# Softmax on one core: two of eight input chunks loaded from ScalarE's store queue, and a larger share of the scaling on ScalarE

## The chip, the cores and the metric

The kernel runs on 1 core of one Trainium2 chip. The metric is the device time of one execution in microseconds (us). Three runs of the kernel before gave 161.81, 161.76 and 161.81 us, so the median is 161.81 us.

## The reference

The input x is float32 of shape 16 x 1024 x 512. The output is a softmax over the last axis with temperature 0.5:

```python
x_scaled = x / 0.5
x_max = np.max(x_scaled, axis=-1, keepdims=True)
exp_x = np.exp(x_scaled - x_max)
return exp_x / np.sum(exp_x, axis=-1, keepdims=True)
```

That is 16384 independent rows of 512 numbers: 33.55 MB are read and 33.55 MB are written.

## The kernel before, in words

**Chunks.** The 16384 rows are cut into eight chunks (`C` = 8) of 128 partitions x `G` = 16 rows, so a chunk is a tile of 128 x 16 x 512 floats, 4096 KB, and each partition's part of it is 32 KB that lie together in memory. Six tiles (`BUFS` = 6) hold chunks; chunks 6 and 7 reuse the tiles of chunks 0 and 1 and can be loaded only after those have been stored. Everything is done in place in these tiles.

**Blocks.** The compute works on blocks of a chunk (`BLOCKS`): chunk 0 is cut in blocks of 4, 4 and 8 rows, chunk 7 in two of 8, and the other chunks are one block of 16 rows. There are eleven blocks. For a block, three engines' queues do this:

- VectorE (DVE) takes the maximum of each row (L77, one instruction for the block) and makes the bias from it (L81). This is the function `shift`.
- ScalarE (ACT) does one instruction per row (L108, `exponentials`), which writes the exponentials in place and their sum into `sums`.
- VectorE inverts the sums (L125) and multiplies the first `k = b - b // 8` of the block's b rows by them (L127, `scale_vector`). ScalarE multiplies the remaining `b // 8` rows, one instruction each (L138, `scale_scalar`). So of 16 rows VectorE scales 14 and ScalarE 2; of 8 rows 7 and 1; of 4 rows 4 and 0.
- When the last block of a chunk is scaled, ScalarE's queue issues the chunk's store (L148, `store`), one DMA of 4096 KB per chunk.

**Loads.** All loads but one small one are issued from SyncE's queue (SP, L68), in the order of the chunks: chunk 0 in two parts of 4 and 12 rows (1024 KB and 3072 KB; "0a" and "0b" below), then chunks 1 to 5 whole, with no wait between them; then chunk 6, which waits until the store of chunk 0 has landed, and chunk 7 without its last row, which waits for the store of chunk 1. The last row of chunk 7 comes from GpSimd's queue (POOL, L97) in two small DMAs.

**Order of work.** The order on each engine is written out by hand (`tc.manual_schedule()`), by the loop at the end of the kernel:

```python
for i in range(n):
    if i + 1 < n:
        exponentials(i + 1, rows(i + 1)[0])
    scale_vector(i)
    scale_scalar(i)
    if i + 2 < n:
        shift(i + 2)
    store(i)
    if i + 1 < n:
        exponentials(i + 1, rows(i + 1)[1])
```

So VectorE does: maximum of block i+1, inverse and scaling of block i, maximum of block i+2, and so on. ScalarE does: the exponentials of block i+1, its share of the scaling of block i, the issue of the store, and the next exponentials. A store that is not ready holds ScalarE. `rows` splits the exponentials of chunk 1 alone: 14 rows come ahead of the store of chunk 0 and 2 rows behind it. A load is issued (on SP, which has nothing else to do) when `shift` first asks for its chunk.

Of the kernel before, what the change touches and what calls it, by code (L numbers as in the profile page):

```python
# [1 line left out]

# [4 lines left out]


@with_exitstack
def kernel(  # L10
    ctx: ExitStack,
    tc: tile.TileContext,
    x: bass.AP,
    out: bass.AP,
):
    nc = tc.nc
    fp32 = mybir.dt.float32
    P = nc.NUM_PARTITIONS
    AX = mybir.AxisListType.X
    EXP = mybir.ActivationFunctionType.Exp  # L20
    COPY = mybir.ActivationFunctionType.Copy
    MAX = mybir.AluOpType.max

    D = x.shape[-1]
    xf = x.flatten_outer_dims()
    of = out.flatten_outer_dims()
    N = xf.shape[0]

    G = 16
    C = N // (P * G)
    assert C * P * G == N
    xr = xf.rearrange("(c p g) d -> c p g d", p=P, g=G)
    outr = of.rearrange("(c p g) d -> c p g d", p=P, g=G)
    WHOLE = [(0, G)]
    LOADS = [[(0, 4), (4, G)]] + [WHOLE] * 6 + [[(0, G - 1)]]
    BLOCKS = [[(0, 4), (4, 8), (8, G)]] + [WHOLE] * 6 + [[(0, 8), (8, G)]]
    STORES = [WHOLE] * 8  # L40
    BMAX = 16
    BUFS = 6

    data = ctx.enter_context(tc.tile_pool(name="data", bufs=BUFS))
    stats = ctx.enter_context(tc.tile_pool(name="stats", bufs=6))

    ctx.enter_context(tc.manual_schedule())


    warm = stats.tile([P, 1], fp32, name="warm", bufs=1)  # L50
    nc.vector.memset(warm, 0.0)  # L51
    nc.scalar.activation(out=warm, in_=warm, func=EXP)  # L52

    chunks = {}
    blocks = [(c, lo, hi) for c in range(C) for lo, hi in BLOCKS[c]]
    n = len(blocks)
    biases, sums, recips = {}, {}, {}

    finished = []

    def load(c):
        if c < BUFS:
            chunks[c] = data.tile([P, G, D], fp32, name="xt")
        else:
            chunks[c] = chunks[c - BUFS]
        xt = chunks[c]
        for lo, hi in LOADS[c]:
            part = nc.sync.dma_start(out=xt[:, lo:hi, :], in_=xr[c][:, lo:hi, :])  # L68
            finished.append(part.ins.name)

    def shift(i):
        c, lo, hi = blocks[i]
        if c not in chunks:
            load(c)
        b = hi - lo
        negmax = stats.tile([P, BMAX], fp32, name="negmax")
        nc.vector.tensor_reduce(  # L77
            negmax[:, 0:b], chunks[c][:, lo:hi, :], axis=AX, op=MAX, negate=True
        )
        biases[i] = stats.tile([P, BMAX], fp32, name="bias")  # L80
        nc.vector.tensor_scalar_mul(biases[i][:, 0:b], negmax[:, 0:b], 2.0)  # L81

    def load_last_row(signal):
        seen = stats.tile([P, 1], fp32, name="seen", bufs=1)
        copied = nc.gpsimd.tensor_copy(out=seen, in_=signal)  # L90
        finished.append(copied.ins.name)
        c = C - 1
        halves = "p (h d) -> p h d"
        to = chunks[c - BUFS][:, G - 1, :].rearrange(halves, h=2)
        of_ = xr[c][:, G - 1, :].rearrange(halves, h=2)
        for p0, p1 in ((P - 2, P), (0, P - 2)):
            part = nc.gpsimd.dma_start(  # L97
                out=to[p0:p1], in_=of_[p0:p1], max_dma_last_dim=2 * D
            )
            finished.append(part.ins.name)  # L100

    def exponentials(i, rows):
        c, lo, hi = blocks[i]
        if i not in sums:
            sums[i] = stats.tile([P, BMAX], fp32, name="sums")
        for g in rows:
            row = chunks[c][:, lo + g, :]
            nc.scalar.activation(  # L108
                out=row,
                in_=row,  # L110
                func=EXP,
                bias=biases[i][:, g : g + 1],
                scale=2.0,
                accum_out=sums[i][:, g : g + 1],
            )
            if c == BUFS - 1 and g == 10:
                load_last_row(sums[i][:, g : g + 1])


    def scale_vector(i):  # L120
        c, lo, hi = blocks[i]
        b = hi - lo
        k = b - b // 8
        recips[i] = stats.tile([P, BMAX], fp32, name="recip")
        nc.vector.reciprocal(recips[i][:, 0:b], sums[i][:, 0:b])  # L125
        rows = chunks[c][:, lo : lo + k, :]
        last = nc.vector.tensor_mul(  # L127
            rows, rows, recips[i][:, 0:k].unsqueeze(2).broadcast_to((P, k, D))
        )
        if i == n - 1:  # L130
            finished.append(last.ins.name)

    def scale_scalar(i):
        c, lo, hi = blocks[i]
        b = hi - lo
        for g in range(b - b // 8, b):
            row = chunks[c][:, lo + g, :]
            last = nc.scalar.activation(  # L138
                out=row, in_=row, func=COPY, scale=recips[i][:, g : g + 1]
            )  # L140
            if i == n - 1:
                finished.append(last.ins.name)

    def store(i):
        c, _, end = blocks[i]
        for lo, hi in STORES[c]:
            if hi == end:
                part = nc.scalar.dma_start(  # L148
                    out=outr[c][:, lo:hi, :], in_=chunks[c][:, lo:hi, :]
                )  # L150
                if c < C - 1:
                    finished.append(part.ins.name)

    shift(0)
    shift(1)

    def rows(i):
        c, lo, hi = blocks[i]
        cut = hi - lo - (2 if c == 1 else 0)
        return range(cut), range(cut, hi - lo)  # L160

    exponentials(0, rows(0)[0])
# [11 lines that stand above are left out]
    seen = nc.sync.nop()  # L174
    info = mybir.DependencyInfo(
        mybir.DependencyClass.Sync, mybir.DependencyReason.DATA
    )
    for name in finished:
        tc.add_manual_dep(seen.ins, name, info, reason="leaves one wait for the end")


# [1 line left out]
_INS = ['x']  # L183
_OUTS = [((16, 1024, 512), 'float32')]


# [23 lines left out]
```

## Time and profile before

| | |
|---|---|
| median of the runs | 161.81 us |
| span of the profiled execution, first to last instruction | 160.5 us |
| time outside the span (median less span) | 1.3 us |
| VectorE busy | 134.6 us (84%), 45 instructions |
| ScalarE busy | 102.2 us (64%), 273 instructions |
| GpSimd busy | 1.9 us |
| moved by DMA | 67.13 MB, 418 GB/s over the span |
| packets of SP's queue, ScalarE's queue, GpSimd's queue | 49.3%, 48.4%, 0.4% of 16 DMA engines' span |
| L77 row maximum, 16 rows | 8.68 us each, six times |
| L127 scaling, 14 rows | 7.62 us each, six times |
| L108 exponentials of a row | 0.708 us, 128 times |
| L138 scaling of a row on ScalarE | 0.706 us, 15 times |

The page of a profile first gives the engines' busy time, then the span in 40 equal slices (each digit is a busy share in tenths), then the DMA queues, the chain of work that ended last, and the costliest groups of instructions. A group's line has the source line, the engine, the operation, output and input with their shapes, the count, the busy time and the mean of one, and then the idle time before it and what ended that. Other views ask the same trace for a stretch of time, for the waits, or for each DMA with its time from issue to landing. DMA engines are not compute engines: the 16 of them serve all queues, and their share stands in a row of its own.

### The profile page before, as it was taken

The page shows a single profiled execution, that of the slowest core. Times are in us where ns is not written, and L with a number is a line of the kernel's source. Part 1 is how long each engine was busy: PE and PEld are TensorE (multiplying, and loading weights), DVE is VectorE, ACT ScalarE, POOL GpSimd, SP SyncE. Part 2 cuts the span into 40 slices and gives each one's busy share as a digit, 9 for nine tenths or more (in the row PEclk, how much of TensorE's full clock was granted, in tenths as well). Part 3 has the DMA queues.
Part 4 walks back from the last instruction along what each step waited for, and adds up shares of the span by engine and source line. Part 5 has one row for each costly group of instructions (what it writes and reads, how often), then busy time and mean ns, then how long its engine had stood idle before and what let it go on. Part 6 is the DMA issues. An engine that isn't in the chain of part 4 may idle for free.

```text
span 160.5 us, 411 instructions
## 1 busy us (share of the span) xinstructions
DVE 134.6 (84%) x45; ACT 102.2 (64%) x273; POOL 1.9 (1%) x7
## 2 busy tenths in 40 slices
DVE  0607999999999999999999999999999999957000
ACT  3071549069989963998199909991899891790000
POOL 0000000000000000000000000030000000000000
DMA  5999999999989999999999999989999999999994
GB/s 184 470 408 498 400 392 457 457 392 402 506 269 425 490 392 400 506 400 392 490 425 392 474 434 392 490 383 483 422 450 400 400 465 441 392 457 449 400 441 204
DMA packets 2578, 67.13 MB, mean 418 GB/s; under 512 B 328, under 2 KB 328, under 8 KB 400
## 3 DMA queue, kind: packets, MB, share of 16 engines
q1 hardware_dynamic: 1296, 33.29, 49.3%
q10 hardware_dynamic: 1152, 33.55, 48.4%
q0 software_dynamic: 128, 0.26, 0.4%
q14 instruction: 2, 0.02, 0.0%
HBM read 33.55 MB, written 33.55 MB: 418 GB/s over the span
## 4 chain that ended last, share of the span: by engine, by line
DVE 75%; DMA 7%; issue 5%; ACT 3%; SPq 0%
DVE negmax L77 42%; DVE xt L127 31%; DMA xt<-in_x_dram 7%; ACT xt L108 3%; DVE bias L81 1%; DVE recip L125 1%; SPq L68 0%
## 5 line engine op out<-in xcount | busy, mean ns | idle before, releaser
L108 ACT ACTIVATE xt<-xt,bias 128x512 f32<-128x512 f32 x128 | 90.4, 708 | 41.5 <-DVE bias L81 40.6
L77 DVE TENSOR_REDUCE negmax<-xt 128x16 f32<-128x8192 f32 (+2 forms) x11 | 69.9, 6352 | 9.4 <-DMA xt<-in_x_dram 9.4
L127 DVE TENSOR_TENSOR xt<-xt,recip 128x7168 f32<-128x7168 f32 (+2 forms) x11 | 62.0, 5637 | 0.4
L108 ACT ACTIVATION_READ_ACCUMULATOR xt<-xt,bias 128x1 f32 x128 | 23.9, 187 | 0.0
L138 ACT ACTIVATE xt<-xt,recip 128x512 f32<-128x512 f32 x15 | 9.9, 706 | 0.0
L125 DVE RECIPROCAL recip<-sums 128x16 f32<-128x16 f32 (+2 forms) x11 | 2.4, 218 | 1.8 <-ACT xt L108 1.8
L81 DVE TENSOR_SCALAR bias<-negmax 128x16 f32<-128x16 f32 (+2 forms) x11 | 1.9, 173 | 0.4
L52 ACT ACT_TABLE_LOAD x1 | 1.3, 1283 | 0.7 <-PEq L194 0.7
L97 POOL DMA_DIRECT2D xt<-in_x_dram x2 | 1.5, 741 | 0.5 <-issue 0.5
L90 POOL COPY seen<-sums 128x1 f32<-128x1 f32 x1 | 0.2, 184 | 103.6 <-ACT xt L108 103.6
L51 DVE MEMSET warm<- 128x1 f32 x1 | 0.1, 59 | 0.8 <-PEq L194 0.8
L52 ACT ACTIVATE warm<-warm 128x1 f32<-128x1 f32 x1 | 0.2, 202 | 0.0
L194 POOL MEMSET const-float32-0.0<- 128x1 f32 x1 | 0.1, 93 | 0.2 <-issue 0.2
L194 POOL MEMSET const-bfloat16-1.0<- 128x1 bf16 x1 | 0.1, 95 | 0.0
L194 POOL MEMSET const-uint8-127<- 128x1 uint8 x1 | 0.1, 95 | 0.0
L194 POOL MEMSET const-float32-1.0<- 128x1 f32 x1 | 0.1, 93 | 0.0
## 6 DMA issues: line engine op xcount, KB each, us to landing
out_dram<-xt ACTq DMA_DIRECT2D x8, 4096.0 KB, 23.1
xt<-in_x_dram SPq DMA_DIRECT2D x6, 4096.0 KB, 34.8
xt<-in_x_dram SPq DMA_DIRECT2D x1, 3840.0 KB, 27.8
xt<-in_x_dram SPq DMA_DIRECT2D x1, 3072.0 KB, 11.6
xt<-in_x_dram SPq DMA_DIRECT2D x1, 1024.0 KB, 4.8
xt<-in_x_dram POOLq DMA_DIRECT2D x1, 252.0 KB, 15.4
xt<-in_x_dram POOLq DMA_DIRECT2D x1, 4.0 KB, 9.1
```

The lines of the kernel that those rows point to most:

```text
L51: nc.vector.memset(warm, 0.0)
L52: nc.scalar.activation(out=warm, in_=warm, func=EXP)
L77: nc.vector.tensor_reduce(negmax[:, 0:b], chunks[c][:, lo:hi, :], axis=AX, op=MAX, negate=True)
L81: nc.vector.tensor_scalar_mul(biases[i][:, 0:b], negmax[:, 0:b], 2.0)
L90: copied = nc.gpsimd.tensor_copy(out=seen, in_=signal)
L97: part = nc.gpsimd.dma_start(out=to[p0:p1], in_=of_[p0:p1], max_dma_last_dim=2 * D)
L108: nc.scalar.activation(out=row, in_=row, func=EXP, bias=biases[i][:, g : g + 1], scale=2.0, accum_out=sums[i][:, g : g + 1],)
L125: nc.vector.reciprocal(recips[i][:, 0:b], sums[i][:, 0:b])
L127: last = nc.vector.tensor_mul(rows, rows, recips[i][:, 0:k].unsqueeze(2).broadcast_to((P, k, D)))
L138: last = nc.scalar.activation(out=row, in_=row, func=COPY, scale=recips[i][:, g : g + 1])
L194: nc = _bacc.Bacc("TRN2", target_bir_lowering=False, num_devices=1)
```

## The change

Three edits:

1. The loads of chunks 1 and 3 move from SP's queue to ScalarE's queue. They are issued there ahead of everything but ScalarE's warm-up, and the first of them waits until 0a (1024 KB) has landed. SP issues 0a, 0b, chunks 2, 4 and 5, and then 6 and 7 with their waits as before. The store of chunk 0 is issued on the queue that now holds the loads of chunks 1 and 3 ahead of it.
2. ScalarE scales `b // 4` rows of a block in place of `b // 8`: of 16 rows VectorE scales 12 and ScalarE 4; of 8 rows 6 and 2; of 4 rows 3 and 1.
3. ScalarE does 6 rows of chunk 1 ahead of the store of chunk 0, and 10 behind it, where it did 14 and 2.

```diff
-    def load(c):
-        if c < BUFS:
-            chunks[c] = data.tile([P, G, D], fp32, name="xt")
-        else:
+    for c in range(BUFS):
+        chunks[c] = data.tile([P, G, D], fp32, name="xt")
+    loaded = set()
+    def load(c, queue):
+        loaded.add(c)
+        if c >= BUFS:
             chunks[c] = chunks[c - BUFS]
         xt = chunks[c]
         for lo, hi in LOADS[c]:
-            part = nc.sync.dma_start(out=xt[:, lo:hi, :], in_=xr[c][:, lo:hi, :])
+            part = queue.dma_start(out=xt[:, lo:hi, :], in_=xr[c][:, lo:hi, :])
+            if c == 1:
+                tc.add_manual_dep(
+                    part.ins, finished[0], data_wait, reason="first rows come alone"
+                )
             finished.append(part.ins.name)

+    load(0, nc.sync)
+    for c in (1, 3):
+        load(c, nc.scalar)
+
     def shift(i):
         c, lo, hi = blocks[i]
-        if c not in chunks:
-            load(c)
+        if c not in loaded:
+            load(c, nc.sync)
...
     def scale_vector(i):
-        k = b - b // 8
+        k = b - b // 4
...
     def scale_scalar(i):
-        for g in range(b - b // 8, b):
+        for g in range(b - b // 4, b):
...
     def rows(i):
         c, lo, hi = blocks[i]
-        cut = hi - lo - (2 if c == 1 else 0)
+        cut = 6 if c == 1 else hi - lo
         return range(cut), range(cut, hi - lo)
```

## The prediction

> **What bounds the kernel now.** I read the page's slices first, then the chain, then the rate of the DMA engines by stretch, then each store's issue and landing.
>
> ```profile
> DVE  0607999999999999999999999999999999957000
> ACT  3071549069989963998199909991899891790000
> ...
> DMA  5999999999989999999999999989999999999994
> ...
> DMA packets 2578, 67.13 MB, mean 418 GB/s; under 512 B 328, under 2 KB 328, under 8 KB 400
> ```
>
> VectorE is full, but so are the DMA engines, and they are the only row that is full to the last slice.
>
> ```profile
> ## 4 chain that ended last, share of the span: by engine, by line
> DVE 75%; DMA 7%; issue 5%; ACT 3%; SPq 0%
> ```
>
> The chain goes back from the last scaling at 147.4 us and puts three quarters on VectorE. It ends 13 us before the span does and is silent about what the last store waits for. The rate by stretch (bytes are booked where a packet starts):
>
> ```profile
> 1.70:44.00 42.30, 33.45 (x15) 22.65 (x63) 0.00 (x0) 1.00 1.02 432
> 44.00:49.00 5.00, 4.93 (x4) 4.28 (x12) 0.00 (x0) 1.00 0.99 334
> 49.00:112.00 63.00, 62.79 (x14) 47.75 (x130) 1.66 (x3) 1.00 0.99 429
> 112.00:149.00 37.00, 33.37 (x14) 26.57 (x70) 0.00 (x0) 1.00 1.01 434
> ```
>
> The last column is GB/s: about 433 with loads alone (to 44 us), with both directions, and with stores alone (from 121 us). So 67.13 MB take 155.0 us, whatever the mix. Data packets run from 1.7 to 159.2 us, 157.5 us in all. Of the 2.5 us over, 1.1 lie in one place: 44 to 49 us, (433 - 334) x 5 = 0.50 MB too little = 1.14 us. The first DMA of ScalarE's queue is issued at 44.1. The packet records there show 32 KB load packets of 2.2 to 2.5 us where others take 1.21, and the first store packets at 48.4 to 49.9. Another 0.7 is the slow first packets, 1.7 to 3 us.
>
> Stores by issue + time to landing: 44.1 + 24.5, 58.95 + 28.9, 75.6 + 31.4, 92.2 + 28.8, 108.8 + 21.7 = 130.5, 125.4 + 14.8 = 140.2, 133.0 + 17.0 = 150.0, 147.5 + 12.2 = 159.7. The last four land 9.7 us apart, which is 4.19 MB at 433 GB/s: stores back to back, no gap. The DMA engines are the bound from end to end. Compute matters only if a store comes too late to follow its predecessor.
>
> How late is too late? Store 7 is issued 2.5 us before store 6 lands, and its packets follow without a gap, from 148.5 (first DMA engine) to 149.5 (last): 1.0 to 2.0 us after the issue. So an issue 2.5 us before the predecessor's landing is surely safe, and up to 1.0 later may be. **Deadlines**: store 5 by 128.0 (130.5 - 2.5) to 129.0; store 6 by 137.7 to 138.7; store 7 by 147.5 to 148.5. Before, they are met by 2.6, 4.7 and 0.
>
> **Edit 1, the loads.** Bytes and packets are the same, so the 155.0 us stay. What can change is the 1.14 us at a second queue's first use, and when chunks land.
>
> *Price of the join.* The trace has one join, of a store to running loads. Here a load joins loads, and the first store later follows on a queue already in use. Bounds: the 1.14 is gone (below: -1.1), or is paid at 5.5 us and again when the first store turns the direction (above: +1.1). A further gain is excluded, as the rate is 433 elsewhere. I take one join, moved from 46 to about 8 us: 0. The nearest row is this join itself.
>
> The Trainium skill speaks against hoping for more: "DMA: Bandwidth & Descriptors", section "Rules for kernel authors", says that spreading DMAs over issuing engines doesn't help bandwidth, as they share 16 DMA engines and it saves issue time only. The row agrees on the rate but shows a join that the rule has no price for; by the rule alone this edit is worth 0 and nothing could be lost. The same page's "Specifications" give about 358 GB/s as a core's share of HBM, which would make 187 us of these bytes; the measured 433 decides.
>
> *Landing.* Before: 0a at 5.5 us (0.7 + 4.8), 0b at 12.8, chunk 1 at 22.5. ScalarE waits for 0a, then issues both loads, done by 6.3 us (0.37 each); its first exponential starts at 8.05, so nothing on ScalarE is held. As at 44.1, the new queue's packets come 5.6 us after the issue, at 11.1. 0b's packets (24 KB, 0.91 us, eight on each DMA engine, from 4.9 us) have then had 6.2 - 1.14 us = 5.5 packets. From there the queues alternate packet by packet, as in the trace, where store 0's eight took 19 us = 16 x 1.21. The other 2.5 take 2.5 x (0.91 + 1.21) = 5.3, so 0b ends at 16.4 and lands (+0.5) at 17. Chunk 1 needs 8 x 1.21 + 2.5 x 0.91 + 5.5 x 1.21 = 18.7 at most: lands at 29 to 30.3. If the new queue starts as early as 8 us, 0b lands at 21 and chunk 1 at 26.5.
>
> *R1*, the start of chunk 1's maximum, was 24.64. It is the later of chunk 1's landing and 0b's landing + 10.8. (From 0b's landing, 12.80, to 24.64 were 11.84; two 4-row scalings lose a row each, 2 x 0.53.) With packets from 11.1: max(27.8, 29.8) = 29.8. From 8: 31.8. Best between: 28.9. I take **29.8**, 5.2 late; range 28.9 to 31.8.
>
> **Edit 2, the rows.** A scaled row costs VectorE (7.62 - 3.89)/7 = 0.533 us, so 12 rows take 6.55 and 6 rows 2.82 + 0.53 = 3.36. The cycle of a chunk falls from 16.62 (37.47 to 54.09) to 15.55. ScalarE gets two more rows, 2 x 0.61 (two take 1.32, the first 0.71). Its idle of 4.0 us per chunk before the next bias covers this: 4.0 - 1.07 - 1.22 = 1.7 left, so VectorE still paces. But these rows stand ahead of the store in ScalarE's queue: a store now comes 21.48 + 1.22 = 22.70 after the next chunk's maximum begins (54.09 to 75.57 before).
>
> **Edit 3** keeps store 0 early: 6 rows of chunk 1 end at R1 + 13.1, two scalings 1.32, store at R1 + 14.4 = 44.2 as before. The ten rows behind it end at R1 + 22.0, while VectorE would ask for their sums at R1 + 21.2: 0.8 lost once. Chunk 3's load ends at about 49 ahead of store 0 in the queue; store 0 then needs 16 x 1.21 and lands near 68.5, as before (68.6), so load 6 (waits for it) and then load 7 (for store 1) keep their times: 96 and 116. They are wanted at 105 and 121.
>
> **The sum.** Chunk 2's maximum starts at R1 + 8.94 + 3.36, chunk 3's at R1 + 28.8, then every 15.55: chunk 6's at R1 + 75.45 (before R1 + 79.3). Store 5: R1 + 75.45 + 22.70 = R1 + 98.15 = **127.95**, deadline 128.0 to 129.0. Store 6: chunk 7's first half gives its bias at R1 + 95.5, but ScalarE comes from store 5 at R1 + 98.55; eight rows 5.64, four scalings 2.54: R1 + 106.8 = **136.6**, deadline 137.7 to 138.7. Store 7: ScalarE is free at R1 + 107.2, eight rows, inverse 0.3, scaling 3.36: R1 + 116.65 = **146.45**, deadline 147.5 to 148.5 (before 147.48). All are met, barely for store 5. VectorE's part ends 1 us earlier and buys nothing, as store 6 is still being written. So the end stays at 160.5 in the span, plus 1.3 outside: **161.8**, the median of before. Its own sum, 160.5 + 1.3, is that median by construction.
>
> **The rivals.** (A measurement of this kernel can tell 0.2%, 0.32 us, from no change.)
> *Faster: the join is free or hidden.* For it: the first store would find its queue in use. Against: a new queue still has to start, now beside 0b. The DMA end comes 1.1 earlier, the deadlines too, and store 5 (with R1 near 29, 127.2 against 126.9 to 127.9) gives up to 0.3 back: 160.7 to 161.2, say 160.9.
> *Slower: store 5 comes late.* If ScalarE's queue gets its packets early (0b starved), R1 is above 30.85 and store 5 passes 129.0; from there each us is a us, since stores 5, 6, 7 need 3 x 9.7 behind it. At R1 = 31.8 store 5 is issued at 129.95, 0.95 to 1.95 late: 162.8 to 163.8. For it: the margin is 0.05 to 1.05 us. Against: at 44.1 the new queue was slow to start, not fast.
> *Slower: two joins*, one at 5.5 us and one when writing begins: 162.9, and the deadlines move back too, so nothing is added.
>
> **Chances.** Forecast 0.42; free join 0.24; store 5 late 0.20; two joins 0.14. So faster by over 0.2%: 0.24; within: 0.42; slower: 0.34. Range: the free join's 160.7 to the two joins' 162.9, and the middle of late store 5, 163.2. The forecast's own range is 161.5 to 162.1.
>
> **What the changed profile will show.** Right: 433 GB/s from 10 us to the end, one dip now near 8 us and none at 46; 0b landing near 17 and chunk 1 near 30; VectorE waiting for DMA about 7 us more at the start; store 5 issued near 128; the last four stores still 9.7 us apart; the last landing near 159.7. Wrong: a landing gap over 9.7 between stores 4 and 5 (late store); a dip left at 46 beside a new one (two joins); no dip at all and a last landing near 158.6 (free join). The forecast also falls if the alternation of queues favours one queue, or if ScalarE and not VectorE sets the cycle.

## The result

Eleven executions of the changed kernel took 162.25 to 163.48 us, median 162.46 us; eleven of the kernel before took 161.75 to 162.17, median 161.91. The ratio is 1.0037, with a 95% interval of 1.0026 to 1.0048: the change costs 0.6 us. Forecast was no change, 161.8.

The profiled execution of the changed kernel has the span that was forecast, 160.5 us. It is also the shortest of its eleven. Each later run lists its time and its span: the time is 1.7 to 1.8 us above the span for both kernels. The spans of before lie between 159.9 and 160.6 (median 160.1 of 82, five of them 160.5 or more), those of the changed kernel between 160.5 and 161.7 (median 160.7 of 11). So the two profiles shown here set a long execution of before beside a short one of the changed kernel, and look alike: by the packet records the median of the 16 DMA engines ends its data at 158.94 us in before and at 158.20 in the changed kernel, but the last at 159.2 in both. The 1.3 us "outside the span" of the first table came from a median and a span of different executions.

### The profile page after: what moved, and what is told of

The parts are those of the page before. It is cut to its first block, busy times and chain, and to the rows that moved or that the text cites. A ratio compares the mean times of both kernels' runs of the same rounds, so it can differ in the third digit from the quotient of the medians.

```text
span 160.5 us, 427 instructions
## 1 busy us (share of the span) xinstructions
DVE 125.7 (78%) x45; ACT 112.5 (70%) x290; POOL 1.9 (1%) x7
## 2 busy tenths in 40 slices
DMA packets 2579, 67.13 MB, mean 418 GB/s; under 512 B 328, under 2 KB 328, under 8 KB 400
## 3 DMA queue, kind: packets, MB, share of 16 engines
q10 hardware_dynamic: 1440, 41.94, 60.6%
q1 hardware_dynamic: 1008, 24.90, 36.7%
## 4 chain that ended last, share of the span: by engine, by line
DVE 56%; ACT 18%; DMA 10%; issue 5%; SPq 0%; ACTq 0%
DVE negmax L91 34%; DVE xt L141 21%; ACT xt L122 17%; DMA xt<-in_x_dram 10%; DVE recip L139 1%; DVE bias L95 1%; ACT xt L152 1%; SPq L74 0%; ACTq L162 0%
## 5 line engine op out<-in xcount | busy, mean ns | idle before, releaser
L141 DVE TENSOR_TENSOR xt<-xt,recip 128x6144 f32<-128x6144 f32 (+2 forms) x11 | 52.9, 4813 | 0.4
L152 ACT ACTIVATE xt<-xt,recip 128x512 f32<-128x512 f32 x32 | 20.5, 706 | 0.0
## 6 DMA issues: line engine op xcount, KB each, us to landing
xt<-in_x_dram SPq DMA_DIRECT2D x1, 3840.0 KB, 28.3
```

The lines of the kernel that those rows point to most:

```text
L141: last = nc.vector.tensor_mul(rows, rows, recips[i][:, 0:k].unsqueeze(2).broadcast_to((P, k, D)))
L152: last = nc.scalar.activation(out=row, in_=row, func=COPY, scale=recips[i][:, g : g + 1])
```

## The profile after

Of the page: the rows of slices of VectorE and of the DMA engines, the count of DMA packets, the DMA queues, and the chain.

```profile
DVE  0600699999997999999999999999999999671000
...
DMA  5999999999999999999999999898999999999993
...
DMA packets 2579, 67.13 MB, mean 418 GB/s; under 512 B 328, under 2 KB 328, under 8 KB 400
...
q10 hardware_dynamic: 1440, 41.94, 60.6%
q1 hardware_dynamic: 1008, 24.90, 36.7%
...
q14 instruction: 3, 0.02, 0.0%
...
## 4 chain that ended last, share of the span: by engine, by line
DVE 56%; ACT 18%; DMA 10%; issue 5%; SPq 0%; ACTq 0%
```

The DMA engines are as full as before. ScalarE's queue (q10) now has 60.6% of their time and SP's (q1) 36.7%. One small number has changed: queue 14, fetches of instructions, has 3 packets in the span where it had 2, and so there are 2579 packets in all for 2578. Fetches are 8 KB each. The row on the page of before:

```profile
q14 instruction: 2, 0.02, 0.0%
```

The rate by stretch, asked as before (last column GB/s):

```profile
5.00:12.00 7.00, 2.46 (x2) 2.93 (x8) 0.00 (x0) 1.00 1.01 434
12.00:44.00 32.00, 26.22 (x13) 16.29 (x43) 0.00 (x0) 1.00 1.01 434
44.00:50.00 6.00, 5.41 (x2) 6.00 (x17) 0.00 (x0) 1.00 0.93 351
```

There is no dip where ScalarE's queue is first used (434 from 5 to 12 us; its loads are issued at 5.4 and 5.9, and their first packets start at 9.2). The dip is still where the first store is issued, 351 in the six microseconds where before had 344.

VectorE's first steps (start, duration, line, operation, and the wait ahead of it):

```profile
17.57 2.29 DVE L91 TENSOR_REDUCE negmax<-xt 128x4 f32<-128x2048 f32 x1 [9.65 <-DMA xt<-in_x_dram]
28.26 8.68 DVE L91 TENSOR_REDUCE negmax<-xt 128x16 f32<-128x8192 f32 x1
40.56 8.68 DVE L91 TENSOR_REDUCE negmax<-xt 128x16 f32<-128x8192 f32 x1
50.36 0.25 DVE L139 RECIPROCAL recip<-sums 128x16 f32<-128x16 f32 x1 [0.92 <-ACT xt L122]
57.12 8.68 DVE L91 TENSOR_REDUCE negmax<-xt 128x16 f32<-128x8192 f32 x1
```

0b's rows are there at 17.57, and chunk 1's maximum starts at 28.3 (R1; the maximum's start shows 0.08 us ahead of the end of the scaling before it). VectorE waits 0.92 us for sums of chunk 1, and the cycle after that is 15.55.

The issues of the last three stores in the timeline of ScalarE (start, duration of the issue):

```profile
126.57 0.34 ACTq L162 DMA_DIRECT2D out_dram<-xt  x1
135.26 0.34 ACTq L162 DMA_DIRECT2D out_dram<-xt  x1
145.11 0.34 ACTq L162 DMA_DIRECT2D out_dram<-xt  x1
```

The DMA issues in three windows around them, one for each (the last column is the time from issue to landing):

```profile
out_dram<-xt ACTq DMA_DIRECT2D x1, 4096.0 KB, 13.2
out_dram<-xt ACTq DMA_DIRECT2D x1, 4096.0 KB, 14.1
out_dram<-xt ACTq DMA_DIRECT2D x1, 4096.0 KB, 14.5
```

They land at 126.57 + 13.2 = 139.8, 135.26 + 14.1 = 149.4 and 145.11 + 14.5 = 159.6. The first gap is 9.6 us, the second 10.2. No store is late: the last was issued 4.3 us before its predecessor landed. Yet it landed 0.5 us late. A landing follows the last of 16 DMA engines: the last packets of these stores end at 139.36, 149.04 and 159.18, each 0.4 us ahead of the landing. So one engine was slower. The third fetch stands in this gap, at 150.2 us. The DMA queues of the changed kernel in the window from 150.1 to 150.7 (packets, time as a share of 16 engines):

```profile
q10 hardware_dynamic: 2, 0.07, 26.9%
q14 instruction: 1, 0.01, 3.2%
```

The packet records say what it costs: 0.31 us for the fetch, and 1.37 us in place of 1.21 for the store packet behind it on that engine, 0.47 us together. Fifteen engines end their data between 157.44 and 158.45 us, and one at 159.18. In before they end between 158.15 and 159.20 with no such gap.

The records don't name a packet's engine, but a packet starts within a few ns of another's end, so they can be linked into 16 chains, one for each engine. Most of these move 4.196 MB, and two move 4.180. All fetches of both kernels lie on one of these two light chains, so this engine has some room: the other light one, without a fetch, ends at 157.44 us in the changed kernel, 0.6 ahead of the next. The three fetches, each with the slower packet behind it, cost 0.55, 0.67 and 0.47 us, 1.69 together, and 157.44 + 1.69 = 159.13 is nearly the 159.18 at which that engine ends. With two fetches, in before, it ends at 158.94, amid the others. So two fetches use up the room, and the third delays the end.

## The experiments

Three theories were set against each other. **P**: ScalarE's program is longer by the 17 scaled rows, and what that brings is the loss (at first taken for time outside the span and a third fetch; after the first four runs as the fetch alone). **S**: a store is late in some executions. **D**: the loads on ScalarE's queue disturb the DMA engines. "Before" in each line is the kernel before on the same chip; it has 305 ScalarE instructions and 2 fetches. The changed kernel has 17 more for the scaled rows, and one more because two loads are issued there and one wait is gone.

| run | ScalarE instructions | fetches in the profiled execution | median us | ratio to before, interval | median span, before's |
|---|---|---|---|---|---|
| changed kernel again | 323 | 3 | 162.41 | 1.0037 (1.0025 to 1.0049) | 160.6, 160.1 |
| rows only | 322 | 3 | 162.75 | 1.0053 (1.0037 to 1.0069) | 160.95, 160.1 |
| loads only | 306 | 2 | 166.13 | 1.0265 (1.0252 to 1.0278) | 164.4, 160.1 |
| 17 idle at the start | 322 | 3 | 162.41 | 1.0040 (1.0024 to 1.0055) | 160.6, 160.1 |
| 3 idle | 308 | 2 | 161.81 | 0.9998 (0.9989 to 1.0007) | 160.05, 160.1 |
| 9 idle | 314 | 2 | 162.13 | 1.0020 (1.0006 to 1.0033) | 160.3, 160.1 |
| 17 idle on VectorE | 305 | 3 | 162.08 | 1.0012 (1.0003 to 1.0020) | 160.3, 160.1 |
| rows on GpSimd | 307 | 2 | 162.31 | 1.0030 (1.0017 to 1.0042) | 160.1, 160.1 |
| fewer on ScalarE | 307 | 2 | 162.24 | 1.0023 (1.0013 to 1.0032) | 160.2, 160.1 |
| early first store | 307 | 2 | 162.10 | 1.0015 (1.0007 to 1.0024) | 160.0, 160.1 |
| 12 idle | 317 | 3, the third after the data | 161.91 | 1.0007 (0.9993 to 1.0022) | 160.15, 160.1 |
| 17 idle at the end | 322 | 3 | 162.48 | 1.0033 (1.0021 to 1.0045) | 160.7, 160.0 |

### The changed kernel again

> The changed kernel as it is, for its spread beside the kernel before on the same chip. Its profiled execution had a span of 160.5 us like before, but 1.75 us outside the span against 1.30. Theory P (the loss comes from ScalarE's longer program: 17 more instructions, a third fetch of instructions, and more time outside the span): every execution again has about 1.75 us outside, the median is 162.4 to 162.5, and the spans spread from 160.5 up. Theory S (a store is late in some executions): the spans and not the time outside carry the loss. Theory D (loads on ScalarE's queue disturb the DMA engines): likewise the spans, by an uneven end of the DMA engines.

Spans 160.5 to 161.0, each 1.8 us below its time; so are those of before. The part of theory P about time outside the span has fallen. In the profiled execution the seventh store lands 10.5 us after the sixth (126.79 + 13.5 = 140.3, 135.48 + 15.3 = 150.8): again the gap in which the third fetch stands (149.6). The eighth lands only 9.4 us after that (145.34 + 14.8 = 160.1), so both gaps together are about 0.5 us longer than two of 9.7.

### Edit 2 alone

```diff
-        k = b - b // 8
+        k = b - b // 4
...
-        for g in range(b - b // 8, b):
+        for g in range(b - b // 4, b):
```

> The kernel before with edit 2 alone: ScalarE scales 4 rows of 16, all loads on SP's queue as before. ScalarE has 17 more instructions. Theory P: about 1.75 us outside the span and 162.2 to 162.5 in all, with the dip at 46 us as before (span 160.5). Theory D: no change, 161.8 to 161.9, and 1.3 outside. Theory S: no change, since VectorE is earlier than before.

0.9 us slower than before, with all loads on SP's queue and VectorE earlier: not D, not S. The seventh store lands 10.2 us after the sixth, with the third fetch at 147.5. It loses more than one fetch is worth: in the profiled execution the last DMA engine is 1.1 us behind the middle one before that fetch, and 1.6 after it. Where the 1.1 come from is open.

### Edit 1 alone

> The changed kernel with edits 2 and 3 undone: the loads of chunks 1 and 3 on ScalarE's queue alone; VectorE scales 14 rows of 16 and 14 rows of chunk 1 come ahead of the first store. Theory P: 1.3 us outside the span. The span has the changed kernel's gain of 0.7 us at 46 us, but the fifth store is now issued near 130 us, 1 to 2 us past its deadline: span 161 to 162.3, 162.3 to 163.6 in all. Theory D: 1.75 us outside, 162.8 to 164.

The edit is the changed kernel with `b // 8` in both places and `cut = hi - lo - (2 if c == 1 else 0)`. 4.3 us slower, more than any theory said. The issues of its last three stores in the timeline of ScalarE:

```profile
130.23 0.34 ACTq L162 DMA_DIRECT2D out_dram<-xt  x1
137.79 0.34 ACTq L162 DMA_DIRECT2D out_dram<-xt  x1
152.28 0.34 ACTq L162 DMA_DIRECT2D out_dram<-xt  x1
```

The same stores in the DMA issues, with their time to landing:

```profile
out_dram<-xt ACTq DMA_DIRECT2D x1, 4096.0 KB, 11.2
out_dram<-xt ACTq DMA_DIRECT2D x1, 4096.0 KB, 13.3
out_dram<-xt ACTq DMA_DIRECT2D x1, 4096.0 KB, 11.1
```

The last store is issued at 152.28, 4.8 us later than before, when its predecessor has already landed at 137.79 + 13.3 = 151.1; it lands at 163.4, 12.3 us behind it and not 9.7. The expectation had looked at the fifth deadline only and forgotten this one. So edit 1 alone delays VectorE by 4.8 us (its last scaling starts at 148.30, before at 143.50) and pays for it, and edits 2 and 3 together buy all of that back. That the deadline of the last store works as the prediction drew it is shown here: 2.5 us before 151.1 is 148.6, up to 1.0 more is free, so 2.7 to 3.7 us were to be lost, and 12.3 - 9.7 = 2.6 were. The rest lies ahead of these stores: the two before the last land 1.1 to 1.2 us later than before, 9.7 us apart. What costs that is open.

### 17 idle instructions on ScalarE

```diff
     nc.scalar.activation(out=warm, in_=warm, func=EXP)
+    for _ in range(17):
+        nc.scalar.activation(out=warm, in_=warm, func=COPY)
```

> The kernel before with 17 more instructions on ScalarE, tiny activations of one element per partition on the warm-up tile, issued while ScalarE waits for the first rows. Nothing else changes. Theory P: about 1.75 us outside the span, a third fetch of instructions, 162.2 to 162.5. Theories S and D: no change, 161.8 to 161.9, 1.3 outside.

These run from 2.3 to 6.2 us, ahead of the first exponential, and no later instruction starts later for them. The time is that of the changed kernel, 162.41. The page's row of queue 14:

```profile
q14 instruction: 3, 0.02, 0.0%
```

The last two stores in the timeline of ScalarE, then in the DMA issues, with their time to landing:

```profile
132.96 0.34 ACTq L150 DMA_DIRECT2D out_dram<-xt  x1
147.44 0.34 ACTq L150 DMA_DIRECT2D out_dram<-xt  x1
...
out_dram<-xt ACTq DMA_DIRECT2D x1, 4096.0 KB, 16.7
out_dram<-xt ACTq DMA_DIRECT2D x1, 4096.0 KB, 12.4
```

Issued at 132.96 and 147.44, they land at 149.6 and 159.8: 10.2 us apart, with the third fetch between (152.9). Neither loads nor scaled rows were touched. S and D cannot explain it.

### Three, nine and twelve

The same loop with 3, 9 and 12.

> The kernel before with 3 idle instructions on ScalarE, where 17 gave 162.41 against 161.85. The fetches of instructions stood where ScalarE had run about 53, 181 and 319 instructions, so some 128 apart; with 3 more ScalarE has 308. Theory P, now narrower (not the number of instructions but one more fetch of 8 KB, which delays the one DMA engine that carries it): two fetches, 161.8 to 161.9, no change. If each instruction costs by itself: 0.1 us, 161.95.

161.81, no change, two fetches, as P said.

> The kernel before with 9 idle instructions on ScalarE, 314 in all. Theory P: a third fetch if 314 is past the step (about 309 to 313 by the spacing), then the whole 0.5 us: 162.3 to 162.5, and one DMA engine that ends 0.6 to 1.0 us behind the rest. If each instruction costs by itself: 0.3 us, 162.15.

0.28 us slower with two fetches: between the two expectations, and neither. The profiled execution (span 160.3) has no late engine; three of the twelve spans are 160.8 to 160.9, the others 159.9 to 160.4.

> The kernel before with 12 idle instructions on ScalarE, 317 in all. With 3 the time was that of before, with 17 it was 0.56 us more with a third fetch, and with 9 it was 0.28 us more though the profiled execution had two fetches. Theory P alone: 161.85 with two fetches or 162.4 with three. If something grows with each instruction past a boundary: about 162.25 with two fetches.

Not slower by the median, but of two kinds: eight spans of 159.9 to 160.3 and four of 160.6 to 161.0. The profiled one is of the latter (160.8). In it the last DMA engine is 1.9 us behind the middle one at the end of the second store and 1.3 at the end of the last, long before any third fetch, which here falls after the last data. So there is a second way in which one engine falls behind. By the linked chains it is the engine that carried the two fetches. With 9 and 12 idle instructions at the start the first two fetches move from 37 and 97 us to 28 and 85. Whether that is what makes the lag in some executions is open.

### 17 idle instructions at the end

```diff
+    for _ in range(17):
+        nc.scalar.activation(out=warm, in_=warm, func=COPY)
     seen = nc.sync.nop()
```

> The kernel before with the 17 idle instructions on ScalarE put behind its last store's issue, where ScalarE has nothing left to do (148 to 152 us). The first two fetches then stay where they are before (near 37 and 97 us; with 9, 12 or 17 idle instructions at the start they moved to 28 and 85 us). Theory P: a third fetch near 150 us, one of the last two stores lands 10.2 us after its predecessor, span median 160.5 to 160.7 against 160.1: 162.2 to 162.45. If the moved first two fetches are what costs: 160.1 and 161.85.

All six spans are 160.5 to 160.8, and the time is 162.48, 0.67 above before by the medians (0.53 by the ratio). The first two fetches are at 37.4 and 97.2 us, as before; the third is at 156.6. The page's row of queue 14:

```profile
q14 instruction: 3, 0.02, 0.0%
```

The issues of the last two stores in the timeline of ScalarE:

```profile
133.09 0.34 ACTq L148 DMA_DIRECT2D out_dram<-xt  x1
147.57 0.34 ACTq L148 DMA_DIRECT2D out_dram<-xt  x1
```

The same two in the DMA issues, with their time to landing:

```profile
out_dram<-xt ACTq DMA_DIRECT2D x1, 4096.0 KB, 16.7
out_dram<-xt ACTq DMA_DIRECT2D x1, 4096.0 KB, 12.4
```

133.09 + 16.7 = 149.8 and 147.57 + 12.4 = 160.0. The last store was issued when it was issued before, and all compute had ended before these instructions ran. What is left is the third fetch, and 0.4 to 0.5 us are seen on the store it meets.

### 17 idle instructions on VectorE

```diff
+    idle = stats.tile([P, 1], fp32, name="idle", bufs=1)
+    for _ in range(17):
+        nc.vector.memset(idle, 0.0)
```

> The kernel before with 17 idle instructions (memsets of one element per partition) on VectorE, while it waits for the first rows. VectorE has 70 instructions then. Theory P: no more fetch, since VectorE's program stays short: two, 161.8 to 161.9. If more instructions anywhere cost (in start or end): 162.4.

The expectation of two fetches was wrong: there is a third one (142.4 us), so a fetch is not ScalarE's alone. The time rises by 0.23 us, less than ScalarE's 0.56; the gap of the seventh store is 9.8 us in this execution. By the linked chains this fetch lies on another engine than the first two, one that was not behind: in this execution it ends at 158.85 us, just behind the other's 158.77.

### The rows on GpSimd

```diff
-        for g in range(b - b // 4, b):
+        for g in range(b - b // 4, b - b // 8):
+            row = chunks[c][:, lo + g, :]
+            moved = nc.gpsimd.tensor_scalar_mul(row, row, recips[i][:, g : g + 1])
+            if i == n - 1:
+                finished.append(moved.ins.name)
+        for g in range(b - b // 8, b):
```

> The changed kernel with the 17 rows that ScalarE took over given to GpSimd instead (the first half of each block's last b // 4 rows), so ScalarE has 306 instructions as without edit 2, and VectorE's share is that of the changed kernel. Theory P: two fetches and 161.7 to 161.9, the time of before, since the loads on ScalarE's queue cost nothing then and the stores come in time (if GpSimd scales a row in under 3 us). Theory D: 162.4, as the loads are still on ScalarE's queue. If GpSimd is slow or slows VectorE, stores are late and the time is above 163, which would leave it open.

The fetches, on the page:

```profile
q14 instruction: 2, 0.02, 0.0%
```

The median span is 160.1, that of before, though the loads are on ScalarE's queue: against D. The time is 162.31, since 2.2 us lie outside the span here and not 1.8; what is outside is not in these traces. A row takes GpSimd 4.2 us on average, and yet the last four stores land 9.7 us apart: none came too late.

### The changed kernel with 16 fewer instructions on ScalarE

```diff
+            if c == 4:
+                nc.gpsimd.memset(sums[i], 1.0)
...
-                accum_out=sums[i][:, g : g + 1],
+                accum_out=None if c == 4 else sums[i][:, g : g + 1],
```

> The changed kernel, but the 16 exponentials of chunk 4 don't write their sums (GpSimd sets that block's sums to 1 with one memset), which takes 16 of ScalarE's instructions away. It leaves out the sums of chunk 4, so that chunk is not normalized; loads, stores and every row's scaling are those of the changed kernel. Theory P (a third fetch of instructions delays the last DMA engine): ScalarE has 307, two fetches, the last stores land 9.7 us apart, span median 160.1 and 161.8 to 161.95 in all, as before. Theory D (the loads on ScalarE's queue): 162.4.

By the span, P: median 160.2, where the changed kernel had 160.6 to 160.7 and before 160.1. Two fetches, by the page's row of queue 14; the last two stores, issued at 135.42 and 145.27, land 9.7 us apart:

```profile
q14 instruction: 2, 0.02, 0.0%
```

The two stores in the timeline of ScalarE, then in the DMA issues, with their time to landing:

```profile
135.42 0.34 ACTq L164 DMA_DIRECT2D out_dram<-xt  x1
145.27 0.34 ACTq L164 DMA_DIRECT2D out_dram<-xt  x1
...
out_dram<-xt ACTq DMA_DIRECT2D x1, 4096.0 KB, 14.0
out_dram<-xt ACTq DMA_DIRECT2D x1, 4096.0 KB, 13.9
```

By the time, neither: 162.24, since 2.07 us lie outside the span in this kernel. The same holds for the next one, 2.08. Why some of these kernels have more there is open. So it is not shown that the time itself returns to that of before without the third fetch.

### The first store split

```diff
-    STORES = [WHOLE] * 8
+    STORES = [[(0, 4), (4, G)]] + [WHOLE] * 7
```

> The kernel before with the store of chunk 0 split: its first 4 rows are stored as soon as they are scaled, near 17.7 us, the other 12 near 44 us as before. This asks what the dip at 46 us is. If it belongs to the first use of ScalarE's queue or to the first write, it moves to about 20 us and none is left at 46. The changed kernel's profile, whose queue is in use from 7 us with the dip still at 46 us, speaks for the first write. No change in the time either way: 161.8 to 161.95. If the dip comes at each beginning of writes beside loads, there are two: 162.5 to 163.

The rate of this kernel by stretch (last column GB/s):

```profile
12.00:20.00 8.00, 7.25 (x5) 2.93 (x8) 0.00 (x0) 1.00 1.07 451
20.00:30.00 10.00, 9.93 (x5) 5.75 (x16) 0.00 (x0) 1.00 0.94 393
30.00:44.00 14.00, 13.93 (x5) 10.59 (x29) 0.00 (x0) 1.00 1.01 436
44.00:50.00 6.00, 5.93 (x4) 5.33 (x15) 0.00 (x0) 1.00 1.00 418
```

The dip is now at 20 to 30 us (393), behind a store issued at 17.7, and 44 to 50 us have 418 and not 344 to 355. Two dips in full there are not; the packet records give about 0.5 us at the first and 0.4 in two small steps up to 60 us, where the other profiles have one of 0.7 to 1.2. With the changed kernel, where loads on the queue run from 9.2 us without a dip, this ties the dip to the first writes beside loads and not to the queue. Edit 1 alone agrees: its queue holds the same loads, its first store is issued only at 48.89, and the dip has moved with it (last column GB/s):

```profile
44.00:50.00 6.00, 6.00 (x1) 5.57 (x16) 0.00 (x0) 1.00 1.01 437
50.00:56.00 6.00, 5.93 (x4) 5.71 (x18) 0.00 (x0) 1.00 0.96 355
```

## Why the prediction was wrong

- *The bound.* Right. The DMA engines are full from end to end, and ScalarE and VectorE matter only through the stores' deadlines, as edit 1 alone shows.
- *Price of the join.* Chosen: one join, moved to 8 us, net 0. The net was right by luck, the place wrong: loads joining loads cost nothing, the first writes still pay at 46 us. All three prices (gone, moved, twice) hung on the queue, and the first store split ties the price to writing.
- *Landing and R1.* 0b was put at 17 us and came at 17.5; chunk 1 at 29 to 30.3, came at 5.4 + 21.8 = 27.2. ScalarE's queue got its first packets 3.8 us after the issue (9.2 for 5.4), not 5.6, so 0b's landing and not chunk 1's set R1: 28.3 for 29.8.
- *Edits 2 and 3, the sum.* The cycle of 15.55, a store 22.7 us after a maximum and the lost 0.8 us (0.92) were right. Stores 5, 6, 7 came at 126.6, 135.3 and 145.1 for 127.95, 136.6 and 146.45, all early by 1.3 to 1.4, R1's error. All deadlines were met, by more than forecast.
- **The step that failed** is in edit 2: "Its idle of 4.0 us per chunk before the next bias covers this". The 17 rows were priced by ScalarE's time alone. They also are 17 instructions, and with them one more 8 KB of instructions is fetched, by one of the DMA engines that are the bound. So "Bytes and packets are the same, so the 155.0 us stay" holds for the data alone, and "the last four stores still 9.7 us apart" fails: the last lands 10.2 us after its predecessor. ScalarE had run 47 to 55 instructions at the first fetch (76 in the changed kernel and the two made from it with two fetches), 176 to 196 at the second, and 319 or 320 at the third, where there was one before the end of the data (295 in the kernel with idle instructions on VectorE). The page of before has this queue in a row of its own, with two packets; the prediction has no term for it. The row's share, 0.0%, is of 16 engines; on the one that ends last a third fetch costs 0.47 us, of the 0.55 that were lost.
- *What is shown and what is not.* That 17 more instructions alone cost 0.56 and 0.67 us is shown by the two runs with 17 idle ones on ScalarE; that 0.5 us of it falls where the third fetch falls, by the gaps of 10.1 to 10.5 us there, in five profiles of four kernels; that it goes away with two fetches, by the spans of the two kernels that keep the loads on ScalarE's queue. By their times it does not: 162.31 and 162.24, with more time outside the span. Open are that time, the 0.28 us with 9 idle instructions, the two kinds of executions with 12, and the 0.3 us by which edit 2 alone exceeds the changed kernel (their intervals overlap): there an engine falls behind by another way as well.
- *The rivals.* No store was late, the join was not paid twice, and it was not free. The slower side was reached by a mechanism that none of them named. The range, 160.7 to 163.2, held the time; the likeliest case did not.
- *The sum's base.* It was made on a span of 160.5, which only five of 82 later executions of before reach. An execution's own span and own time belong together.

The Trainium skill, "Runtime: NRT & Kernel Launch", section "Instruction fetch mechanics", says that instructions are refilled in 16 KiB blocks of 256 instructions by the sequencer's own DMA queue, and that crossing a block is mostly hidden. Here the packets are of 8 KB and come some 100 to 145 instructions apart, and the cost is not hidden where that DMA engine is what ends last.

None of the kernels was faster than before beyond its interval. The changed kernel without its third fetch would be as fast as before at best, by the spans.

## What to carry to other kernels

Where the DMA engines are the bound, every byte on the last engine counts, also those that no line of the kernel moves: count the instructions a change adds to an engine, and look at the queue of instruction fetches before and after. The landing of back-to-back transfers is a clock for this: a gap that grows by half a microsecond with no late issue is a sign that one of the 16 engines had other work. Two such fetches went unseen here and the third did not, since the engine that carried them had a little less data than the others. And before a profile is used as the base of a small difference, its execution's time has to be placed among the others'.

## What the runs showed of the hardware that was not expected

- A fetch of 8 KB of instructions mostly takes a DMA engine 0.31 us, and the 32 KB packet behind it takes 1.33 to 1.59 in place of 1.21 us. In before and in the changed kernel all fetches lie on one DMA engine; the one that came with 17 more VectorE instructions lies on another.
- Loads from a second queue joined running loads at 434 GB/s, with no loss; the first writes beside loads cost 0.7 to 1.2 us once, in every profile but the one with an early small store.
- A GpSimd scaling of a 128 x 512 row took 3.1 us in some places and 4.7 in others, and a pair of rows 9.5 us, once 3.1, while VectorE's durations (6558 ns for 12 rows) stayed the same.
- The time outside the span was 1.8 us for most kernels and 2.07 to 2.22 us for three of them.
